# Reciprocal square roots by a GpSimd power: two LayerNorms and the output norm of a delta rule

## The chip, the cores and the metric

The kernel runs on one core of one Trainium2 chip. The metric is the device time of one execution in microseconds (us), as the median of several runs. In what follows PE is TensorE (matrix multiplications), PEld its weight loads, DVE is VectorE, ACT is ScalarE, POOL is GpSimd, and SP is SyncE, which issues nearly all DMA transfers.

## The reference, cut to what matters

One inference step of a two-layer hybrid encoder on 2048 prompt rows and 32 sample rows of width 1024. Layer 1 is a gated delta rule with 8 heads of 128, layer 2 a windowed attention with 16 query heads that share 4 key/value heads. The three places that the change concerns are the norm of the delta rule's output, per token and head, and the LayerNorm behind each layer's output projection:

```python
def layer_norm(x, g, b):
    xf = x.astype(jnp.float32)
    mu = xf.mean(-1, keepdims=True)
    var = jnp.square(xf - mu).mean(-1, keepdims=True)
    return ((xf - mu) * lax.rsqrt(var + LN_EPS) * g + b).astype(x.dtype)
...
    o, s_new = gated_delta_rule(q, k, v, g, beta, s0.astype(jnp.float32))
    o = o * lax.rsqrt(jnp.mean(o * o, -1, keepdims=True) + RMS_EPS) * norm_w * jax.nn.silu(z.astype(jnp.float32))
    out = o.reshape(b, l, A_VW).astype(x.dtype) @ w_out
    return layer_norm(DN_ALPHA * x + out, ln_g, ln_b), new_buf, s_new.astype(x.dtype)
...
    out = (o * jax.nn.silu(z)) @ w_out
    return layer_norm(DN_ALPHA * x + out, ln_g, ln_b)
```

The delta rule is solved exactly in blocks: each block needs the inverse of a unit lower triangular matrix per head, and its outputs depend on the state S that the block before left.

## The kernel before, in words

All rows are worked on in 17 tiles: 16 of 128 prompt rows and one of the 32 sample rows. Matrix products that need full accuracy are split into a high and a low part and done in three passes (lines L77 to L79 for the projections, L1089 to L1091 for the output projections); the low part of an activation or of a weight (act_lo L69, w_lo L54, g_lo L1132 and L1456) is a subtraction on POOL or VectorE.

The stages, in the order of time in the profiled execution:

- **Projection P1** (0 to about 690 us): q, k, v by blocks of 416 rows, a short convolution, and the row norms of q and k. That norm (`norms`, L423) uses the Newton iteration too and is not changed.
- **Delta rule** (class `Delta`, `run` at L803; about 690 to 1160 us): 17 chunks, one iteration of the loop over i per chunk and some 25 us each. While chunk i is finished, chunk i+1 gets its triangular inverse completed and chunk i+2 is prepared. The triangular solve of a 32x32 part is a chain of 31 steps j, each one multiplication (`tm`, L585) and one subtraction (`Tt`, L588) of small tiles: for j = 0 to 24 they run on POOL for chunk i+2 (`chain(n2, P, 0, n2.split)`), and in the next iteration VectorE does j = 25 to 30, then `spread` (L656, L657) and `invert` (L680 to L705). The state update `Sp` (L761, VectorE) stands between VectorE's chain steps, and PE's `ks` (L714) reads the new state. The output norm of chunk i is `norms` (L774): `Xo` (L778) is the mean square plus epsilon, [128 rows, 8 heads], then eleven VectorE operations give its reciprocal root `ro_y`, and `scale` (L787) multiplies the output o by it. `run` hands out the eleven one by one with `go(... r ...)` between other VectorE work such as `at` (L630) and `E` (L542). Matrix products of the remaining projection are filled in between (`fill`) until iteration 10; from iteration 11 (`OPEN`) the output projection takes their place in pieces (`side`).
- **Output projection O1** (class `OutNorm`, `tile` at L1135; most of it about 1138 to 1372 us): per tile two times 24 products of 512 columns, the residual added (L1097), `bn_stats` and `bn_aggr`, the variance plus epsilon `ve` (L1153, [128, 1]), eleven operations for `ln_y`, then two pairs of operations for the two halves of the tile: L1165 subtracts the mean and multiplies by the gain, L1167 multiplies by `ln_y` and adds the bias. PE transposes the result r (L1194) during the products of the next tile, and the copy `hT` (L1196) and a DMA put it away for the next projection.
- **Projection P2** (about 1372 to 1776 us) with the rotary embedding, and **attention** (about 1776 us to the end): per chunk scores `S` (L1559), a softmax whose exponentials P are made on ACT (L1442) and multiplied on POOL (L1567), transposes (L1574), the output products `ot` (L1580), and `finish` (L1449): output projection, `ve` (L1473), eleven Newton operations, `nb` (L1477, VectorE), r times rstd plus nb on ACT (L1478), then gain and bias on POOL (L1479, L1480) and the DMA to the output (L1488). For the very last tile, the gain and bias steps are on VectorE instead (L1484, L1486).

The Newton iteration for the reciprocal square root is eleven operations that each need the one before:

```python
    V.tensor_scalar(out=y[:n].bitcast(I32), in0=x[:n].bitcast(I32), scalar1=1, scalar2=None,
                    op0=ALU.logical_shift_right)
...
    V.tensor_scalar(out=y[:n].bitcast(I32), in0=y[:n].bitcast(I32), scalar1=-1, scalar2=0x5F3759DF,
                    op0=ALU.mult, op1=ALU.add)
...
    for _ in range(3):
        V.scalar_tensor_tensor(out=t[:n], in0=x[:n], scalar=-0.5, in1=y[:n], op0=ALU.mult, op1=ALU.mult)
        V.tensor_tensor(out=t[:n], in0=t[:n], in1=y[:n], op=ALU.mult)
        V.scalar_tensor_tensor(out=y[:n], in0=t[:n], scalar=1.5, in1=y[:n], op0=ALU.add, op1=ALU.mult)
```

What sets the order: every engine works through its own list in order and waits at each instruction for the semaphores of its inputs. In the delta rule and O1 the lists of PE and VectorE (and ACT's in the delta rule) are as `run` and `tiles` write them. POOL's and SP's lists, and all lists of the attention, are put in order by a scheduler when the program is built. A changed instruction can therefore move others on POOL, SP and ACT.

Of the kernel before, what the change touches and what calls it, by code (L numbers as in the profile page):

```python
# [10 lines left out]
F32 = mybir.dt.float32  # L11
# [3 lines left out]
ALU = mybir.AluOpType  # L15
# [416 lines left out]
def newton_steps(nc, pool, x, y, n, w, tag):  # L432

    V = nc.vector
    t = pool.tile([128, w], F32, tag=tag + "_t", name=tag + "_t")
    V.tensor_scalar(out=y[:n].bitcast(I32), in0=x[:n].bitcast(I32), scalar1=1, scalar2=None,
                    op0=ALU.logical_shift_right)
    yield
    V.tensor_scalar(out=y[:n].bitcast(I32), in0=y[:n].bitcast(I32), scalar1=-1, scalar2=0x5F3759DF,
                    op0=ALU.mult, op1=ALU.add)  # L440
    yield
    for _ in range(3):
        V.scalar_tensor_tensor(out=t[:n], in0=x[:n], scalar=-0.5, in1=y[:n], op0=ALU.mult, op1=ALU.mult)
        yield
        V.tensor_tensor(out=t[:n], in0=t[:n], in1=y[:n], op=ALU.mult)
        yield
        V.scalar_tensor_tensor(out=y[:n], in0=t[:n], scalar=1.5, in1=y[:n], op0=ALU.add, op1=ALU.mult)
        yield


def rsqrt_newton(nc, pool, x, n, w, tag):
    y = pool.tile([128, w], F32, tag=tag + "_y", name=tag + "_y")
    drain(newton_steps(nc, pool, x, y, n, w, tag))
    return y


class Chunk:
    def __init__(self, t0, n):
        self.t0, self.n, self.ti, self.ready, self.pool = t0, n, t0 // 128, False, None
# [3 lines left out]
class Delta:  # L463
# [310 lines left out]
    def norms(self, ch):  # L774


        V, n, X = self.nc.vector, ch.n, ch.X
        V.scalar_tensor_tensor(out=X[:n], in0=X[:n], scalar=1.0 / 128, in1=self.G["eq"][:n, ch.ti, :], op0=ALU.mult,  # L778
                               op1=ALU.add)
        yield  # L780
        ch.r = self.two.tile([128, 8], F32, tag="ro_y", name="ro_y")
        yield from newton_steps(self.nc, self.sml, X, ch.r, n, 8, "ro")

    def scale(self, ch):
        n = ch.n
# [318 lines left out]
class OutNorm:  # L1104


    def __init__(self, tc, es, name, side, I, pre, banks, kept):
        self.nc = nc = tc.nc
        self.one = new_pool(tc, es, name + "_one", 1, side=side)
        self.two = new_pool(tc, es, name + "_two", 2, side=side)  # L1110
        self.pp = new_pool(tc, es, name + "_pp", banks, PSUM, side=side)
        self.tabs = None
        self.tables = lambda: ln_tables(nc, self.one, I[pre + "_ln_g"], I[pre + "_ln_b"])
        self.rest = load_part_weights(nc, self.one, self.two, I[pre + "_w_out"], kept, nc.vector)
        self.w = next(self.rest)
# [19 lines left out]
    def tile(self, parts, r, n, tail=False):  # L1135

        nc, V = self.nc, self.nc.vector
        ghi, glo = parts
        st = self.two.tile([128, 2, 6], F32, tag="st", name="st")
        w = self.w  # L1140
        for c in range(2):
            cs = slice(c * 512, c * 512 + 512)
            ps = self.pp.tile([128, 512], F32, tag="po", name="po")
            for k in range(KC):
                out_products(nc, ps, ghi, glo, w, k, cs, n)
                if k % 2 == 1:
                    yield (4 if n <= 64 else 6) * 0.227
            add_products(nc, r, glo, ps, cs, n)
            V.bn_stats(out=st[:n, c, :], in_=r[:n, cs])
        mv = self.two.tile([128, 2], F32, tag="mv", name="mv")  # L1150
        V.bn_aggr(out=mv[:n], in_=st[:n])
        ve = self.two.tile([128, 1], F32, tag="ve", name="ve")
        V.tensor_scalar(out=ve[:n], in0=mv[:n, 1:2], scalar1=LN_EPS, scalar2=None, op0=ALU.add)  # L1153
        rs = rsqrt_newton(nc, self.two, ve, n, 1, "ln")
        tabs = self.tabs
        if not tail:
            nb = self.two.tile([128, 1], F32, tag="nb", name="nb")
            V.scalar_tensor_tensor(out=nb[:n], in0=mv[:n, 0:1], scalar=-1.0, in1=rs[:n], op0=ALU.mult, op1=ALU.mult)
            nc.scalar.activation(r[:n], r[:n], AF.Identity, bias=nb[:n, 0:1], scale=rs[:n, 0:1])
            nc.gpsimd.tensor_tensor(out=r[:n], in0=r[:n], in1=tabs[0][:n], op=ALU.mult)  # L1160
            nc.gpsimd.tensor_tensor(out=r[:n], in0=r[:n], in1=tabs[1][:n], op=ALU.add)
        else:
            for c in range(2):
                cs = slice(c * 512, c * 512 + 512)
                V.scalar_tensor_tensor(out=r[:n, cs], in0=r[:n, cs], scalar=mv[:n, 0:1], in1=tabs[0][:n, cs],  # L1165
                                       op0=ALU.subtract, op1=ALU.mult)
                V.scalar_tensor_tensor(out=r[:n, cs], in0=r[:n, cs], scalar=rs[:n, 0:1], in1=tabs[1][:n, cs],  # L1167
                                       op0=ALU.mult, op1=ALU.add)
        yield r


class O1:
    def __init__(self, tc, es, I, O, T, G):
        self.nc, self.I, self.T, self.G = tc.nc, I, T, G
        self.on = OutNorm(tc, es, "o1", "left", I, "a", 2, T["wo"])
        self.bank = lambda: self.on.pp.tile([128, 512], F32, tag="po", name="tr")
        self.steps = 0
        self.room = lambda: self.on.one.tile([128, KC, 128], F32, tag="g", name="hT")
# [196 lines left out]
class Attention:  # L1375
# [73 lines left out]
    def finish(self, t0, n, graw, late=False, tail=False):  # L1449
        nc, V, pool = self.nc, self.nc.vector, self.otwo  # L1450
        r = pool.tile([128, D], F32, tag="r", name="r")
        nc.sync.dma_start(r[:n], self.T["h"][t0:t0 + n, :])
        ghi = pool.tile([128, KC, 128], F32R, tag="g_hi", name="g_hi")
        glo = pool.tile([128, KC, 128], F32R, tag="g_lo", name="g_lo")
        nc.scalar.copy(ghi[:, :, :n], graw[:, :, :n])
        nc.gpsimd.tensor_tensor(out=low_part(ghi, glo, n), in0=graw[:, :, :n], in1=ghi[:, :, :n], op=ALU.subtract)  # L1456
        st = pool.tile([128, 2, 6], F32, tag="st", name="st")
        w, tabs = self.w, self.tabs
        both = self.scores_tile() if late else None
        for c in range(2):  # L1460
            cs = slice(c * 512, c * 512 + 512)
            if late:
                ps = both[:, c].rearrange("p u k -> p (u k)")
            else:
                ps = self.pp.tile([128, 512], F32, tag="po", name="po")[:]
            for k in range(KC):
                out_products(nc, ps, ghi, glo, w, k, cs, n)
            add_products(nc, r, glo, ps, cs, n)
            V.bn_stats(out=st[:n, c, :], in_=r[:n, cs])
        mv = pool.tile([128, 2], F32, tag="mv", name="mv")  # L1470
        V.bn_aggr(out=mv[:n], in_=st[:n])
        ve = pool.tile([128, 1], F32, tag="ve", name="ve")
        V.tensor_scalar(out=ve[:n], in0=mv[:n, 1:2], scalar1=LN_EPS, scalar2=None, op0=ALU.add)  # L1473
        rs = rsqrt_newton(nc, pool, ve, n, 1, "ln")
        if not tail:
            nb = pool.tile([128, 1], F32, tag="nb", name="nb")
            V.scalar_tensor_tensor(out=nb[:n], in0=mv[:n, 0:1], scalar=-1.0, in1=rs[:n], op0=ALU.mult, op1=ALU.mult)  # L1477
            nc.scalar.activation(r[:n], r[:n], AF.Identity, bias=nb[:n, 0:1], scale=rs[:n, 0:1])  # L1478
            nc.gpsimd.tensor_tensor(out=r[:n], in0=r[:n], in1=tabs[0][:n], op=ALU.mult)  # L1479
            nc.gpsimd.tensor_tensor(out=r[:n], in0=r[:n], in1=tabs[1][:n], op=ALU.add)  # L1480
        else:
            for c in range(2):
                cs = slice(c * 512, c * 512 + 512)
                V.scalar_tensor_tensor(out=r[:n, cs], in0=r[:n, cs], scalar=mv[:n, 0:1], in1=tabs[0][:n, cs],  # L1484
                                       op0=ALU.subtract, op1=ALU.mult)
                V.scalar_tensor_tensor(out=r[:n, cs], in0=r[:n, cs], scalar=rs[:n, 0:1], in1=tabs[1][:n, cs],  # L1486
                                       op0=ALU.mult, op1=ALU.add)
        nc.sync.dma_start(self.O["y"][t0:t0 + n, :], r[:n])  # L1488
# [244 lines left out]
def make_consts(tc, I, pool):  # L1733
    nc = tc.nc
    G = {}
    G["ident"] = pool.tile([128, 128], F32, tag="ident", name="ident")
    nc.sync.dma_start(G["ident"][:], I["ident"])
    for name in ("hn", "eq", "ekd", "egl", "ngc"):
        G[name] = pool.tile([128, NTT, H], F32, tag=name, name="t_" + name)
    return G  # L1740
# [126 lines left out]
```

## Time and profile before

| | |
|---|---|
| time, median of 3 runs | 2205.87 us (2204.95 to 2206.77) |
| the profiled execution's own time | 2205.77 us |
| span of its instructions | 2204.0 us |
| mean granted TensorE clock | 0.989 |
| busy: PE, VectorE, ScalarE, GpSimd | 98%, 62%, 42%, 38% of the span |

The span runs from the first instruction to the last; what lies around it is 1.8 us here. A row of a timeline reads: start, duration, engine, line, operation, output <- inputs, shape, and in brackets the idle time of the engine just before, with what ended it. Matrix products are pipelined and their ends are modelled, so a PE that counts as busy isn't always at its peak.

### The profile page before, as it was taken

How to read it: one execution, taken by the hardware profiler on the slowest of the kernel's cores; microseconds unless marked ns; L12 is line 12 of the kernel's file. 1: busy time of each engine (PE TensorE's matmuls, PEld its weight loads, DVE VectorE, ACT ScalarE, POOL GpSimd, SP SyncE). 2: the span in 40 equal slices, each digit the busy share in tenths (PEclk: the TensorE clock that was granted, in tenths of full speed). 3: DMA queues.
4: the chain of work that ended last, by engine and by line, in shares of the span. 5: the costliest groups of instructions: out<-in, count | busy, mean ns of one | idle time of the engine just before them, and what ended most of it. 6: DMA issues, size and time to landing. Idle time of an engine off the chain costs nothing.

```text
span 2204.0 us, 36640 instructions
## 1 busy us (share of the span) xinstructions
PE 2152.8 (98%) x13706; PEld 1984.2 (90%) x13706; DVE 1372.1 (62%) x2696; ACT 917.4 (42%) x2303; POOL 843.1 (38%) x1189
## 2 busy tenths in 40 slices
PE   8999999999999999999999999999999999999997
PEld 6999999999999899998888788999999986788884
DVE  3676666754366688888868875135442236668774
ACT  4444344433323677877831213222112245444541
POOL 1422212222211378878811201056441215556563
PEclk9999999999999999999999999999999999999999
DMA  5212222333354344447427764374221287233311
GB/s 197 68 59 79 67 78 68 99 110 95 107 156 144 101 148 137 133 131 238 165 94 220 224 194 145 98 239 161 68 74 66 85 197 236 79 103 97 106 63 53
DMA packets 250530, 274.48 MB, mean 125 GB/s; under 512 B 76096, under 2 KB 195200, under 8 KB 250080
## 3 DMA queue, kind: packets, MB, share of 16 engines
q1 hardware_dynamic: 238352, 248.84, 37.0%
q10 hardware_dynamic: 12000, 23.30, 3.0%
q8 instruction: 108, 1.77, 0.3%
q14 instruction: 70, 0.57, 0.1%
HBM read 168.53 MB, written 103.92 MB: 124 GB/s over the span
## 4 chain that ended last, share of the span: by engine, by line
PE 89%; POOL 3%; DMA 3%; DVE 2%; ACT 2%; issue 1%; ACTq 0%; SPq 0%; DVEq 0%; POOLq 0%
PE ps L77 17%; PE ps L79 17%; PE ps L78 17%; PE po L1089 5%; PE po L1091 5%; PE po L1090 5%; PE ot L1580 4%; PE S L1559 2%; PE tr L1574 2%; POOL Tt L588 1%; POOL tm L585 1%; PE g L562 1%; PE vp L725 1%; PE op L739 1%; PE ks L714 1%
## 5 line engine op out<-in xcount | busy, mean ns | idle before, releaser
L77 PE MATMUL ps<-act_hi,w_hi 128*128 128x416 f32 x2000 | 706.3, 354 | 2.7 <-ACT w_hi L53 1.5
L79 PE MATMUL ps<-act_hi,w_lo 128*128 128x416 f32 x2000 | 704.5, 353 | 2.4 <-POOL w_lo L54 1.2
L78 PE MATMUL ps<-act_lo,w_hi 128*128 128x416 f32 x2000 | 701.2, 351 | 0.2 <-DVE act_lo L69 0.2
L77 PEld LDWEIGHTS ps<-act_hi,w_hi 128*128 128x128 f32 x2000 | 376.6, 188 | 7.8 <-ACT w_hi L53 2.4
L79 PEld LDWEIGHTS ps<-act_hi,w_lo 128*128 128x128 f32 x2000 | 375.8, 188 | 7.2 <-POOL w_lo L54 1.7
L78 PEld LDWEIGHTS ps<-act_lo,w_hi 128*128 128x128 f32 x2000 | 376.1, 188 | 5.1 <-DVE act_lo L69 0.9
L54 POOL TENSOR_TENSOR w_lo<-w_raw,w_hi 128x1024 fp32r<-128x1024 f32 x44 | 117.0, 2660 | 472.3 <-ACT w_hi L53 446.2
L196 DVE SCALAR_TENSOR_TENSOR y<-R,convw,y 128x2083 f32<-128x2083 f32 x72 | 173.7, 2414 | 109.4 <-ACT y L194 85.0
L585 POOL TENSOR_TENSOR tm<-L,Tt 128x60 f32<-128x60 f32 (+19 forms) x373 | 139.3, 374 | 89.8 <-PE sp L755 42.9
L1567 POOL TENSOR_TENSOR P<-P,sm 128x384 f32<-128x384 f32 (+2 forms) x128 | 101.6, 814 | 177.6 <-DVE sm L1446 100.6
L588 POOL TENSOR_TENSOR Tt<-Tt,tm 128x60 f32<-128x60 f32 (+19 forms) x373 | 157.2, 421 | 29.2
L1442 ACT ACTIVATE P<-S,nm 128x192 f32<-128x192 f32 (+2 forms) x260 | 104.7, 419 | 94.2 <-DVE nm L1435 41.4
L227 ACT COPY R<-ps 128x416 f32<-128x416 f32 (+1 forms) x144 | 61.2, 448 | 197.5 <-PE ps L79 173.0
L1089 PE MATMUL po<-wo_hi,g_hi 128*128 128x512 f32 x256 | 104.8, 410 | 1.8 <-ACT hT L1196 1.8
L1286 POOL TENSOR_TENSOR rs<-rs,sin 128x416 f32<-128x416 f32 x50 | 71.1, 1421 | 80.0 <-DVE rs L1285 73.4
L1090 PE MATMUL po<-wo_lo,g_hi 128*128 128x512 f32 x256 | 101.1, 395 | 0.0
L1091 PE MATMUL po<-wo_hi,g_lo 128*128 128x512 f32 x256 | 101.0, 395 | 0.0
L1580 PE MATMUL ot<-pt,vd 128*128 128x256 f32 x372 | 98.7, 392 | 1.9 <-ACT pt L1576 1.4
L1089 PE MATMUL po<-wo,g_hi 128*128 128x512 f32 x240 | 99.4, 414 | 0.0
L53 ACT CAST w_hi<-w_raw 128x1024 fp32r<-128x1024 f32 x48 | 50.3, 1049 | 116.8 <-PE ps L78 88.2
L1091 PE MATMUL po<-wo,g_lo 128*128 128x512 f32 x240 | 96.2, 401 | 0.0
L1090 PE MATMUL po<-wo,g_hi 128*128 128x512 f32 x240 | 96.1, 400 | 0.0
(306 smaller groups left out, 4024.2 us busy)
## 6 DMA issues: line engine op xcount, KB each, us to landing
w_raw<-in_w_in SPq DMA_DIRECT2D x40, 512.0 KB
w_raw<-in_b_w_in SPq DMA_DIRECT2D x20, 512.0 KB
gb<-s_gcum SPq DMA_DIRECT2D x17, 512.0 KB
k<-s_k SPq DMA_DIRECT2D x17, 512.0 KB
s_bz<-za SPq DMA_DIRECT2D x40, 208.0 KB
s_bq<-ra SPq DMA_DIRECT2D x40, 208.0 KB
s_q<-y SPq DMA_DIRECT2D x8, 1024.0 KB
s_k<-y SPq DMA_DIRECT2D x8, 1024.0 KB
```

The costliest lines, as they stand in the source:

```text
L54: sub.tensor_tensor(out=lo[:], in0=raw[:], in1=hi[:], op=ALU.subtract)
L77: nc.tensor.matmul(ps, hi[:, k, :], xh[:, k, :], start=(k == 0), stop=False)
L78: nc.tensor.matmul(ps, hi[:, k, :], xl[:, k, :], start=False, stop=False)
L79: nc.tensor.matmul(ps, lo[:, k, :], xh[:, k, :], start=False, stop=(k == KC - 1))
L196: nc.vector.scalar_tensor_tensor(out=y[:], in0=R[:, j:j + W], scalar=self.convw[:, i, j:j + 1], in1=y[:], op0=ALU.mult, op1=ALU.add)
L585: P.tensor_tensor(out=tm[:n, i0 - k:, :w], in0=L[:n, i0:, j:j + 1].to_broadcast(sh), in1=Tt[:n, j:j + 1, :w].to_broadcast(sh), op=ALU.mult)
L588: P.tensor_tensor(out=Tt[:n, i0:, :w], in0=Tt[:n, i0:, :w], in1=tm[:n, i0 - k:, :w], op=ALU.subtract)
L1089: nc.tensor.matmul(ps[:n], ghi[:, k, :n], w[0][:, k, cs], start=a, stop=False)
L1090: nc.tensor.matmul(ps[:n], ghi[:, k, :n], w[1][:, k, cs], start=False, stop=False)
L1091: nc.tensor.matmul(ps[:n], glo[:, k, :n], w[0][:, k, cs], start=False, stop=z)
L1442: nc.scalar.activation(P[u], src, AF.Exp, bias=nm[:, u:u + 1], scale=1.0, accum_out=sm[:, u:u + 1])
L1580: nc.tensor.matmul(ot[:, p], self.vd[:, kc0 + j, p, :], pt[:, 2 * j:2 * j + 2, :], start=(j == 0), stop=(j == nj - 1))
```

## The change: what it does

A function `root` is added, one GpSimd operation that raises x to the power -0.5. The exponent comes from a tile `half` that is filled once at the start. Three callers use it in place of the Newton iteration: `Delta.norms` (17 times, [128, 8]), `OutNorm.tile` (17 times, [128, 1]) and `Attention.finish` (17 times, [128, 1]). So 51 x 11 VectorE operations go and 51 POOL operations come. In the delta rule the result is no longer handed out in steps: the later `go(r)` calls of `run` find an empty generator. The tile's name changes from `ln_y` to `rs` in the two LayerNorms; in the delta rule it stays `ro_y`. The Newton iteration of P1's `norms` stays.

```diff
+def root(nc, G, out, x):
+
+    nc.gpsimd.tensor_tensor(out=out, in0=x, in1=G["half"][:x.shape[0], 0:x.shape[1]], op=ALU.pow)
...
         V.scalar_tensor_tensor(out=X[:n], in0=X[:n], scalar=1.0 / 128, in1=self.G["eq"][:n, ch.ti, :], op0=ALU.mult,
                                op1=ALU.add)
+        ch.r = self.two.tile([128, 8], F32, tag="ro_y", name="ro_y")
+        root(self.nc, self.G, ch.r[:n], X[:n])
         yield
-        ch.r = self.two.tile([128, 8], F32, tag="ro_y", name="ro_y")
-        yield from newton_steps(self.nc, self.sml, X, ch.r, n, 8, "ro")
...
         V.tensor_scalar(out=ve[:n], in0=mv[:n, 1:2], scalar1=LN_EPS, scalar2=None, op0=ALU.add)
-        rs = rsqrt_newton(nc, self.two, ve, n, 1, "ln")
+        rs = self.two.tile([128, 1], F32, tag="rs", name="rs")
+        root(nc, self.G, rs[:n], ve[:n])
...
         V.tensor_scalar(out=ve[:n], in0=mv[:n, 1:2], scalar1=LN_EPS, scalar2=None, op0=ALU.add)
-        rs = rsqrt_newton(nc, pool, ve, n, 1, "ln")
+        rs = pool.tile([128, 1], F32, tag="rs", name="rs")
+        root(nc, self.G, rs[:n], ve[:n])
...
+    G["half"] = pool.tile([128, H], F32, tag="half", name="half")
+    nc.gpsimd.memset(G["half"][:], -0.5)
```

The second and third pair are those of `OutNorm.tile` and of `Attention.finish`; `OutNorm` also gets G handed in by `O1`.

More of the change, by code (lines that the diff above doesn't have):

```diff
@@ L1104, with __init__ @@
 class OutNorm:
-    def __init__(self, tc, es, name, side, I, pre, banks, kept):
-        self.nc = nc = tc.nc
+    def __init__(self, tc, es, name, side, I, pre, banks, kept, G):
+        self.nc, self.G = tc.nc, G
+        nc = tc.nc
         self.one = new_pool(tc, es, name + "_one", 1, side=side)
@@ L1174, in __init__ @@
         self.nc, self.I, self.T, self.G = tc.nc, I, T, G
-        self.on = OutNorm(tc, es, "o1", "left", I, "a", 2, T["wo"])
+        self.on = OutNorm(tc, es, "o1", "left", I, "a", 2, T["wo"], G)
         self.bank = lambda: self.on.pp.tile([128, 512], F32, tag="po", name="tr")
```

## The prediction, made before the changed kernel was run

> **What bounds the kernel now.** I read the page first, then the windows by stage, the chain of waits inside the delta rule, and the timelines of VectorE (DVE) and GpSimd (POOL) where the change cuts in. The page:
>
> ```profile
> span 2204.0 us, 36640 instructions
> ...
> PE 2152.8 (98%) x13706; PEld 1984.2 (90%) x13706; DVE 1372.1 (62%) x2696; ACT 917.4 (42%) x2303; POOL 843.1 (38%) x1189
> ...
> PE 89%; POOL 3%; DMA 3%; DVE 2%; ACT 2%; issue 1%; ACTq 0%; SPq 0%; DVEq 0%; POOLq 0%
> ```
>
> TensorE sets the end nearly everywhere, so 51 x 11 small VectorE operations removed are worth nothing as busy time. The 3% of POOL on the chain of waits matters more, since POOL receives the new work. The windows (columns: busy time of PE, PEld, DVE, ACT, POOL, then the TensorE clock) say where each stands:
>
> ```profile
> 865.00:890.00 25.00, 25.00 (x274) 23.99 (x274) 22.00 (x52) 20.02 (x63) 19.75 (x49) 1.00 0.44 136
> 1015.00:1040.00 25.00, 23.87 (x276) 22.52 (x274) 20.98 (x50) 21.62 (x71) 20.48 (x54) 1.00 0.61 197
> 1040.00:1065.00 25.00, 22.33 (x248) 21.30 (x248) 21.23 (x52) 20.26 (x62) 20.87 (x53) 0.93 0.61 199
> 1065.00:1090.00 25.00, 20.86 (x248) 19.69 (x248) 21.65 (x55) 20.95 (x70) 20.91 (x53) 1.00 0.61 214
> 1860.00:2000.00 140.00, 139.22 (x759) 109.25 (x759) 95.52 (x275) 64.94 (x251) 79.17 (x66) 1.00 0.32 87
> 2000.00:2150.00 150.00, 150.00 (x857) 122.06 (x854) 118.57 (x322) 74.91 (x286) 92.02 (x75) 1.00 0.30 87
> ```
>
> In delta iterations 0 to 10 (first row, one iteration of 25 us) PE is full. In 11 to 14 it is not, up to 4.1 us short per 25. What holds it there, by the chain of waits for 1005 to 1110 and by the waits of 1010 to 1115 (total, times, longest):
>
> ```profile
> by line: POOL Tt L588 29.6%; POOL tm L585 28.8%; issue 10.0%; PE vp L725 5.2%; PE ks L714 2.7%; PE gq L629 2.3%; ACT kd L601 2.0%; PE g L562 1.9%; ACT nb L567 1.4%; PE vtr L612 1.4%; ACT vn L771 1.2%; ACT vn L615 1.1%; PE bps L686 1.0%; PE
> ```
> ```profile
> PE ks L714 <- DVE Sp L761: 6.0, 4, 2.0
> DVE tm L585 <- POOL Tt L588: 5.7, 4, 1.7
> ```
>
> POOL's 25-step solve (L585/L588) runs chain after chain; VectorE's last steps wait for its end, the state update Sp is queued behind those on VectorE, and PE waits for Sp. A POOL instruction added here moves the end.
>
> **Part 1: the delta rule's output norm (17 times, [128,8]).** Iteration 6 and the start of 7 on POOL, and the VectorE row that needs the chain:
>
> ```profile
> 868.45 0.26 POOL L585 TENSOR_TENSOR tm<-L,Tt 128x31 f32<-128x31 f32 x1 [1.57 <-ACT vn L771]
> ...
> 871.15 0.30 POOL L588 TENSOR_TENSOR Tt<-Tt,tm 128x28 f32<-128x28 f32 x1
> ...
> 892.36 0.29 POOL L588 TENSOR_TENSOR Tt<-Tt,tm 128x49 f32<-128x49 f32 x1
> 893.50 0.26 POOL L585 TENSOR_TENSOR tm<-L,Tt 128x31 f32<-128x31 f32 x1 [0.85 <-DVE tm L585]
> ```
> ```profile
> 893.24 0.17 DVE L585 TENSOR_TENSOR tm<-L,Tt 128x42 f32<-128x42 f32 x1
> ```
>
> In the changed program's POOL order the power stands inside the chain: after its 14th pair in iterations 1 to 10, within the 11th pair in 11 to 14, after all chains in 15 and 16. Its price is in no row. Below I put 0.25 us, since the smallest POOL TENSOR_TENSOR here lasts 0.26 to 0.30; above 3.3 us, as if POOL did the eleven steps one by one at 0.30. I take 1.0 us for 128x8, near the middle of these two ends in ratio (the square root of 0.25 x 3.3 is 0.9), and 0.55 for 128x1; with the gap of about 0.07 between POOL instructions, 1.07.
>
> Iterations 0 to 10: the chain of iteration 6 ends at 892.65, and VectorE takes it at 893.24. The two idle gaps, 1.57 and 0.85, average 1.21 us per iteration. 1.07 fits, narrowly: **0**. Above a price of about 1.15 us it no longer does, and POOL becomes the bound of all eleven iterations.
>
> Iterations 11 to 14:
>
> ```profile
> 1024.03 0.14 DVE L778 SCALAR_TENSOR_TENSOR Xo<-Xo,t_eq 128x8 f32<-128x8 f32 x1
> ...
> 1024.94 0.28 DVE L436 TENSOR_SCALAR ro_y<-Xo 128x8 int32<-128x8 int32 x1
> ...
> 1026.17 1.37 DVE L542 TENSOR_TENSOR E<-gb,nm 128x1024 f32<-128x1024 f32 x1
> ...
> 1028.61 1.23 DVE L787 TENSOR_TENSOR o<-o,ro_y 128x1024 f32<-128x1024 f32 x1
> ```
> ```profile
> 1017.14 0.26 POOL L585 TENSOR_TENSOR tm<-L,Tt 128x31 f32<-128x31 f32 x1 [0.45 <-ACT vn L771]
> ...
> 1026.53 1.18 POOL L585 TENSOR_TENSOR tm<-L,Tt 128x76 f32<-128x76 f32 x1
> ```
>
> VectorE loses 1028.61-1024.94-1.37 = 2.3 us of Newton steps, but it waits for POOL later in the iteration anyway: worth 0. The power's input is written at 1024.03, before its place in the chain, so POOL does not wait for it. Only 0.45 us of idle time stands before the chain of iteration 11, so iteration 10's power carries 1.07-0.45 = **+0.6** into it; the chains of 11, 12 and 13 add 1.07 each, **+3.2**; that of 14 is partly covered, because PE's own late sp is waited for next: **+0.5**. Sum +4.3.
>
> The second POOL row shows a cost that stays: beside E on VectorE it lasts 1.18 us where its neighbours last 0.3. The Trainium skill, "SBUF — State Buffer", section "SBUF: two separate sides", says that GpSimd and a VectorE operation with two SBUF inputs hold a shared pair of ports exclusively, the other blocking fully. The trace agrees (1.18 against 0.3); by that rule a power caught behind E, o or k could last some 0.9 us longer, an estimate that would make the delta sum about +7.
>
> **Part 2: LayerNorm of the output projection (17 times, [128,1]).** Tile 2, where the P2 weight split also sits on POOL:
>
> ```profile
> 1173.23 0.14 DVE L1153 TENSOR_SCALAR ve<-mv 128x1 f32<-128x1 f32 x1
> ...
> 1175.34 0.16 DVE L447 SCALAR_TENSOR_TENSOR ln_y<-ln_t,ln_y 128x1 f32<-128x1 f32 x1
> ...
> 1177.64 0.75 DVE L1167 SCALAR_TENSOR_TENSOR r<-r,ln_y,ln_b 128x512 f32<-128x512 f32 x1
> 1178.31 1.22 DVE L1132 TENSOR_TENSOR g_lo<-g,g_hi 128x1024 fp32r<-128x1024 f32 x1
> ...
> 1179.85 2.40 POOL L54 TENSOR_TENSOR w_lo<-w_raw,w_hi 128x1024 fp32r<-128x1024 f32 x1 [67.85 <-ACT w_hi L53]
> ```
> ```profile
> 1180.95 0.60 PE L1194 MATMUL ps<-ident,r 128*128 128x128 f32 x4
> ```
>
> In the new POOL order w_lo stands ahead of tile 2's power. It waits for its data until 1179.85 and lasts 2.40, so the power can't start before 1182.3 although ve is ready at 1173.4. Root at 1182.9, the first half of r at 1183.7, all of it at about 1185.1 instead of 1178.4; g_lo and the add that frees a PSUM bank are queued behind it on VectorE. PE's transposes of r, at 1180.95 now, start 2.7 (first half enough) to 4.2 us late: **+3.5**. Tile 3's power stands behind the second w_lo, beside which one Newton step lasts 2.3 us already: even. Tile 5's stands behind an activation split on POOL; PE's second transposes of that tile wait today:
>
> ```profile
> 1216.20 2.27 POOL L69 TENSOR_TENSOR act_lo<-act_raw,act_hi 128x832 fp32r<-128x832 f32 x1 [3.05 <-ACT act_hi L68]
> ```
> ```profile
> 1219.16 0.63 PE L1194 MATMUL ps<-ident,r 128*128 128x128 f32 x4 [0.75 <-DVE r L1167]
> ```
> ```profile
> 1240.00:1372.00 132.00, 131.44 (x655) 112.03 (x655) 97.36 (x224) 30.01 (x47) 14.13 (x9) 1.00 0.58 180
> ```
>
> The split ends at 1218.5, root at 1219.1, r at 1221.3: 2 us behind today's transposes if the split moves along with tile 2's delay, and nothing if it does not, as PE is then 3.5 us later itself: **+1**. From 1240 on PE is full, POOL nearly idle: 0. Sum +4.5.
>
> **Part 3: LayerNorm of the attention (17 times) and the tail.** From 2000 to 2150 PE is full. From 1860 to 1930 the chain of waits is:
>
> ```profile
> by line: PE ot L1580 21.8%; PE S L1559 17.4%; PE po L1089 14.8%; PE po L1090 13.6%; PE po L1091 13.3%; PE tr L1574 12.2%; DVE nm L1435 2.4%; ACT P L1442 2.4%; DVE nm L1434 1.4%; ACT pt L1576 0.7%; issue 0.5%; ACTq L1442 0.1%
> ```
>
> VectorE and ScalarE hold 6.3% of 70 us, 4.4 us, of which a shorter VectorE queue may give back some: I take **-1**. The bound is what 1860 to 2000 would save at the weight-load density of 2000 to 2150: 140 - 109.25/(122.06/150) = 5.7 us. On the other side, nb waits on VectorE for a power that may stand behind POOL's products; at one 2.4 us POOL instruction a time in the two or three chunks not yet full of PE, up to +5.
>
> The tail, on POOL, SP and VectorE:
>
> ```profile
> 2175.36 2.38 POOL L1456 TENSOR_TENSOR g_lo<-graw,g_hi 128x1024 fp32r<-128x1024 f32 x1
> 2177.70 2.84 POOL L1480 TENSOR_TENSOR r<-r,ln_b 128x1024 f32<-128x1024 f32 x1
> ...
> 2183.26 0.32 SPq L1452 DMA_DIRECT2D r<-s_h  x1
> ...
> 2195.33 0.15 DVE L1473 TENSOR_SCALAR ve<-mv 128x1 f32<-128x1 f32 x1
> 2195.40 1.40 DVE L1484 SCALAR_TENSOR_TENSOR r<-r,mv,ln_g 128x512 f32<-128x512 f32 x2
> 2196.72 0.14 DVE L436 TENSOR_SCALAR ln_y<-ve 128x1 int32<-128x1 int32 x1
> ...
> 2198.83 1.42 DVE L1486 SCALAR_TENSOR_TENSOR r<-r,ln_y,ln_b 128x512 f32<-128x512 f32 x2
> ```
>
> At the end, the power runs beside L1484 (1.40) instead of 2.1 us of Newton after it: -1.4 after a handover, up to -2. Earlier, the last chunk's g_lo moves behind the two POOL steps of the chunk before, so r<-s_h can be issued sooner: about -1.5. **-2.9** (0 to -4).
>
> **Sum.** +4.3 +4.5 -1 -2.9 = +4.9, on the profiled execution's 2205.77 us, which agrees with the median of 2205.87: **2210.7 us**.
>
> **Rivals.**
> A. The power costs 2 us or more, and POOL bounds the whole delta rule. Against the 1.21 us of idle time: 11 x (2.07-1.21) = 9.5, iterations 11 to 14 with the carry 3.5 x 2.07+0.7 = 8, O1 5, tail -1.5: +21, 2227; at 3.3 us, 23.8+12.5+6.5-0.5 = +42, 2248. For it: a power is no multiply, and no row prices it. Against: 2 us for 8 columns is nearly seven times what POOL takes for a product of 28 (0.30). A sentence apart: the Trainium skill, "GPSIMD Engine Reference", section "Instruction dispatch", gives about 6 us for the first call of a freshly loaded kernel; no run here shows it, and it would add an estimated 5 us once.
> B. The other side: attention is relieved in full (-5.7), the tail gives -3.5, a power of 0.35 us costs the delta 3.5 x 0.42 = +1.5, and w_lo's data come early enough that tile 2 pays nothing: 2198. It decides by whether PE's weight loads in 1860 to 2000 become as dense as later, 0.81 busy against 0.78. Against it: PE already counts as busy for 139.22 of 140.
> C. It cancels: a power near 0.5 us (delta +2), tile 2 at +2.7, tail -3.5, attention 0: about 2207.
>
> **How the numbers follow.** What the measurement can tell from no change is about 0.2%, 4.4 us: 2201.5 to 2210.3, and my sum lies just above its upper edge. Chances: forecast with its own range 2206 to 2217, 0.38; A 0.27; B 0.13; C 0.22. Above the bound lie all of A, some 0.22 of the forecast's case and 0.01 of C: slower 0.50. Below lie B and 0.05 of C: faster 0.18. The rest: same 0.32. The range reaches into B and A: 2199 to 2236.
>
> **What would show it.** The POOL rows of the power give its price. In iterations 11 to 14, chain starts on POOL should stand 1.0 us or so further apart than 24; in 0 to 10 the period should stay 25.0 (wider: A). PE's transposes of tile 2 should wait 3 to 4 us, with w_lo ahead of the power. The weight-load share of 1860 to 2000 decides B. In the tail, the last L1484 and L1486 should follow each other closely. The forecast is wrong if the price misses 0.6 to 1.2 us, or if PE's waits appear where I saw it full.

## The result, and the profile after

| | median | runs |
|---|---|---|
| before | 2205.41 us | 2204.21 to 2206.77 (4) |
| changed | 2223.50 us | 2221.95 to 2228.78 (4) |

The ratio is 1.0083 (1.0066 to 1.0100): the change costs 18.1 us. The profiled execution of the changed kernel is the slowest of its four (2228.78 us, mean TensorE clock 0.987), so the stage lengths are shown from a second profile of it too, that of e1 (2221.46 us, 0.992).

The page of the changed kernel, the lines that answer to those of before:

```profile
span 2227.0 us, 36148 instructions
...
PE 2166.9 (97%) x13706; PEld 1987.5 (89%) x13706; DVE 1282.7 (58%) x2135; ACT 918.0 (41%) x2303; POOL 881.7 (40%) x1241
...
PE 84%; POOL 5%; DMA 4%; DVE 3%; ACT 2%; issue 2%; SPq 1%; ACTq 0%; DVEq 0%; POOLq 0%
```

VectorE lost 89 us of busy time, and PE's share of the chain fell from 89% to 84%: the removed work was hardly on the path, and waits came onto it. The power itself, grouped by shape:

```profile
L459 POOL TENSOR_TENSOR rs<-ve,half x34: 540/547/992, 1142.8 to 2220.7; 128x1 f32<-128x1 f32 x32, 32x1 f32<-32x1 f32 x2
...
L459 POOL TENSOR_TENSOR ro_y<-Xo,half x17: 1637/1647/2729, 752.9 to 1159.1; 128x8 f32<-128x8 f32 x16, 32x8 f32<-32x8 f32 x1
```

(Numbers after the colon: shortest, median, longest in ns, then first and last start.) 1.65 us for eight columns, 0.55 for one: if a straight line holds between these two sizes, some 0.16 us a column on a base of 0.39 (an estimate). I had assumed 1.0 and 0.55.

Where the time went is read from the same VectorE rows in each trace: `Xo` of the delta rule, and `ve` of the two LayerNorms, whose first and last starts group as follows, before and then changed:

```profile
L1153 DVE TENSOR_SCALAR ve<-mv x17: 141/153/155, 1138.5 to 1345.5; 128x1 f32<-128x1 f32 x16, 32x1 f32<-32x1 f32 x1
```
```profile
L1159 DVE TENSOR_SCALAR ve<-mv x17: 142/154/156, 1142.6 to 1358.4; 128x1 f32<-128x1 f32 x16, 32x1 f32<-32x1 f32 x1
...
L1480 DVE TENSOR_SCALAR ve<-mv x17: 132/147/154, 1879.2 to 2220.4; 128x1 f32<-128x1 f32 x16, 32x1 f32<-32x1 f32 x1
```

| stretch (us) | before | changed | changed, e1 | alone |
|---|---|---|---|---|
| delta, Xo of iteration 10 to 16 | 152.3 | 155.3 | 152.6 | 153.1 (e2) |
| O1, first ve to last | 207.0 | 215.9 | 215.1 | 214.6 (e3) |
| attention, 7th ve to 13th | 130.0 | 137.6 | 137.6 | 137.6 (e4) |
| 13th ve to the end | 71.7 | 69.3 | 69.2 | 69.3 (e4) |

Kernels whose delta rule is that of before show 148.7 to 152.5 in the first row, so a single profile can't price that stage to better than some 3 us; the timed runs do. Most of this spread lies in the last of the six intervals: 22.7 us in the five of these profiles whose granted clock was 1.00 from 1128 to 1155 us, 25.9 to 27.2 in the four where it was 0.87 or 0.88 there (before is one of these). In the second row, kernels with Newton in O1 show 204.5 to 207.6, so before's own 207.0 lies high; the third row is clear. In O1 the power waits behind other POOL work. POOL of the changed kernel, and the VectorE rows of tiles 2, 5 and 8 that use the root:

```profile
1181.64 2.66 POOL L54 TENSOR_TENSOR w_lo<-w_raw,w_hi 128x1024 fp32r<-128x1024 f32 x1 [16.83 <-ACT w_hi L53]
1184.25 0.55 POOL L459 TENSOR_TENSOR rs<-ve,half 128x1 f32<-128x1 f32 x1
...
1220.16 1.98 POOL L69 TENSOR_TENSOR act_lo<-act_raw,act_hi 128x832 fp32r<-128x832 f32 x1 [3.25 <-ACT act_hi L68]
1222.10 0.54 POOL L459 TENSOR_TENSOR rs<-ve,half 128x1 f32<-128x1 f32 x1
...
1260.92 1.98 POOL L69 TENSOR_TENSOR act_lo<-act_raw,act_hi 128x832 fp32r<-128x832 f32 x1 [2.77 <-ACT act_hi L68]
1262.86 0.54 POOL L459 TENSOR_TENSOR rs<-ve,half 128x1 f32<-128x1 f32 x1
```
```profile
1184.84 0.75 DVE L1174 SCALAR_TENSOR_TENSOR r<-r,rs,ln_b 128x512 f32<-128x512 f32 x1 [2.79 <-POOL rs L459]
...
1222.68 0.75 DVE L1174 SCALAR_TENSOR_TENSOR r<-r,rs,ln_b 128x512 f32<-128x512 f32 x1 [5.22 <-POOL rs L459]
...
1263.43 0.75 DVE L1174 SCALAR_TENSOR_TENSOR r<-r,rs,ln_b 128x512 f32<-128x512 f32 x1 [4.73 <-POOL rs L459]
```

The bracket is VectorE idle: 2.8, 5.2 and 4.7 us, with the add (L1102) that frees PE's PSUM bank queued behind each. The other tiles wait 0.44 or 0.45 us.

In the attention no such wait explains 7.6 us; PE's own order is another. The score products S of before and of the changed kernel, on PE:

```profile
2040.15 1.57 PE L1559 MATMUL S<-kT,qs 64*128 64x192 f32 x16
2041.65 1.56 PE L1580 MATMUL ot<-pt,vd 128*128 128x256 f32 x6
```
```profile
2058.77 0.59 PE L1567 MATMUL S<-kT,qs 64*128 64x192 f32 x4
2059.30 0.55 PE L1582 MATMUL tr<-ident,P 128*128 128x128 f32 x3
```

From S to the next instruction: 16 records in 1.50 us, 94 ns each, before; 4 in 0.53 us, 133 ns each, after. In the list that the scheduler wrote for PE, and in PE's rows of the traces, the score products of the prompt's chunks stand in 53 unbroken groups before and in 68 after.

### The profile page after: what moved, and what is told of

Its sections match the earlier page's. It is cut to its first block, busy times and chain, and to the rows that moved or that the text cites. A ratio compares the mean times of both kernels' runs of the same rounds, so it can differ in the third digit from the quotient of the medians.

```text
span 2227.0 us, 36148 instructions
## 1 busy us (share of the span) xinstructions
PE 2166.9 (97%) x13706; PEld 1987.5 (89%) x13706; DVE 1282.7 (58%) x2135; ACT 918.0 (41%) x2303; POOL 881.7 (40%) x1241
## 4 chain that ended last, share of the span: by engine, by line
PE 84%; POOL 5%; DMA 4%; DVE 3%; ACT 2%; issue 2%; SPq 1%; ACTq 0%; DVEq 0%; POOLq 0%
PE ps L77 17%; PE ps L79 16%; PE ps L78 16%; PE po L1094 4%; PE po L1096 4%; PE po L1095 4%; PE ot L1588 4%; PE S L1567 2%; POOL tm L590 2%; POOL Tt L593 2%; DMA act_raw<-s_hT 2%; PE tr L1582 2%; PE g L567 1%; PE vp L730 1%; PE op L744 1%
## 5 line engine op out<-in xcount | busy, mean ns | idle before, releaser
L590 POOL TENSOR_TENSOR tm<-L,Tt 128x60 f32<-128x60 f32 (+19 forms) x373 | 133.9, 359 | 76.6 <-ACT vn L776 44.8
L593 POOL TENSOR_TENSOR Tt<-Tt,tm 128x60 f32<-128x60 f32 (+19 forms) x373 | 149.1, 400 | 28.8
```

What stands on the lines that cost most here:

```text
L590: P.tensor_tensor(out=tm[:n, i0 - k:, :w], in0=L[:n, i0:, j:j + 1].to_broadcast(sh), in1=Tt[:n, j:j + 1, :w].to_broadcast(sh), op=ALU.mult)
L593: P.tensor_tensor(out=Tt[:n, i0:, :w], in0=Tt[:n, i0:, :w], in1=tm[:n, i0 - k:, :w], op=ALU.subtract)
```

## The experiments

All were timed in turn with the kernel before on the same chip. The table gives each median, that of before beside it, and the ratio with its 95% interval.

| | kernel | median | before | ratio |
|---|---|---|---|---|
| e1 | the whole change again | 2223.15 | 2204.53 | 1.0080 (1.0067 to 1.0094) |
| e2 | delta rule alone | 2207.65 | 2204.53 | 1.0011 (1.0002 to 1.0020) |
| e3 | O1 alone | 2214.63 | 2204.53 | 1.0039 (1.0025 to 1.0053) |
| e4 | attention alone | 2210.08 | 2204.53 | 1.0026 (1.0016 to 1.0037) |
| e5 | last three LayerNorms of the attention | 2197.01 | 2205.48 | 0.9967 (0.9954 to 0.9980) |
| e6 | attention with no root at all | 2215.67 | 2205.48 | 1.0057 (1.0037 to 1.0077) |
| e7 | attention: Newton, and a power unused | 2203.44 | 2205.48 | 0.9996 (0.9984 to 1.0008) |
| e8 | O1 but for tiles 2, 5, 8 | 2205.45 | 2205.48 | 1.0002 (0.9993 to 1.0012) |
| e9 | delta rule, power doubled | 2215.62 | 2207.33 | 1.0048 (1.0030 to 1.0066) |
| e10 | delta rule with no root | 2205.06 | 2207.33 | 0.9993 (0.9981 to 1.0005) |
| e11 | O1 with no root | 2202.09 | 2207.33 | 0.9978 (0.9968 to 0.9988) |
| e12 | first six and last three of the attention | 2198.27 | 2207.33 | 0.9959 (0.9943 to 0.9975) |

**The three parts (e1 to e4).** In each, the two other places go back to Newton, for instance

```diff
-        rs = self.two.tile([128, 1], F32, tag="rs", name="rs")
-        root(nc, self.G, rs[:n], ve[:n])
+        rs = rsqrt_newton(nc, self.two, ve, n, 1, "ln")
```

> The whole change once more, on the same chip as its three parts. About 2222 us if the first profiled execution (2228.8) was a few us above the others; the three parts should then sum to about +17 if they are independent.

> The power in the delta rule alone, Newton in both LayerNorms. Theory 1, from the offsets of the changed trace: nothing in iterations 0 to 10 although the power takes 1.65 us, because it covers one of the blocked 1.18 us steps, and +3 in 11 to 16: about 2209. Theory 2, the rival A of the prediction: POOL is the bound of all iterations, 11 x (1.72-1.21) more: about 2215.

> The power in the output projection's LayerNorm alone. Theory 1: three powers (tiles 2, 5, 8) wait behind w_lo and act_lo on POOL, PE loses 1.5+1.8+4 there and 1 to 2 where the next projection starts: about 2214. Theory 2, the loss came from upstream delays that meet the weights' DMA: less than half of it, about 2208.

> The power in the attention's LayerNorm alone. Its order of PE breaks the score products into 68 groups where before has 53. Theory 1: this order costs what the changed trace lost between 2027 and 2131, about 9 us, and the tail gives 3.6 back: about 2211. Theory 2: that loss was a wait handed down from upstream or a clock that differed in that one execution, and only the tail's gain is left: about 2202.

By the ratios on 2205 us the parts cost 2.4 (0.4 to 4.4), 8.6 (5.5 to 11.7) and 5.7 us (3.5 to 8.2), 16.7 together, against 17.6 for the whole: they add up, and the times are those of theory 1 in each. POOL is not the bound of the early delta iterations, O1 is the largest part, and the attention costs by itself, on an undisturbed start. In one thing e3 is not as expected: its tile 2 pays next to nothing. VectorE's rows for tiles 2, 5 and 8, and PE's two long waits, in e3:

```profile
1175.39 0.75 DVE L1174 SCALAR_TENSOR_TENSOR r<-r,rs,ln_b 128x512 f32<-128x512 f32 x1 [0.44 <-POOL rs L459]
...
1213.12 0.75 DVE L1174 SCALAR_TENSOR_TENSOR r<-r,rs,ln_b 128x512 f32<-128x512 f32 x1 [4.97 <-POOL rs L459]
...
1254.05 0.75 DVE L1174 SCALAR_TENSOR_TENSOR r<-r,rs,ln_b 128x512 f32<-128x512 f32 x1 [4.99 <-POOL rs L459]
```
```profile
1218.96 0.47 PE L1094 MATMUL po<-wo_hi,g_hi 128*128 128x512 f32 x1 [2.54 <-DVE r L1102]
...
1259.90 0.47 PE L1094 MATMUL po<-wo_hi,g_hi 128*128 128x512 f32 x1 [2.54 <-DVE r L1102]
```

Here w_lo started at 1172.00, so tile 2's power came at 1174.36 and VectorE waited 0.44 us for it. With 1.04 and 0.87 us before the transposes of tiles 5 and 8, PE's idle time at these two tiles is 7.0 us.

**O1: is it the queue? (e8, e11)**

```diff
-        rs = self.two.tile([128, 1], F32, tag="rs", name="rs")
-        root(nc, self.G, rs[:n], ve[:n])
+        if newton:
+            rs = rsqrt_newton(nc, self.two, ve, n, 1, "ln")
+        else:
+            rs = self.two.tile([128, 1], F32, tag="rs", name="rs")
+            root(nc, self.G, rs[:n], ve[:n])
...
-            for j, out in enumerate(self.on.tile(got, r, t[2], True)):
+            for j, out in enumerate(self.on.tile(got, r, t[2], True, i in (2, 5, 8))):
```

> As the power in the output projection alone, but Newton for tiles 2, 5 and 8, whose powers stood behind w_lo or act_lo. Theory 1, these three waits are the loss: 6 to 8 of the 8.6 us come back, about 2206. Theory 2, the power's own handover (0.9 to 1.2 us a tile against 2.1 of Newton) or the shifted DMAs cost: 2212 or more.

All of it came back, within 2 to 3 us. The wait of VectorE for the root falls from 16 us in O1 alone to 6 with three Newton tiles (total, times, longest; e3, then e8):

```profile
DVE r L1174 <- POOL rs L459: 16.2, 16, 5.0
```
```profile
DVE r L1177 <- POOL rs L459: 5.8, 13, 0.5
```

So these three of seventeen powers made the loss, and the other fourteen gained nothing that the interval shows (0.9993 to 1.0012). e8 changes the three together; by the waits in e3 it was two of them, tiles 5 and 8. e11 takes both forms away (`rs = ve`), the most that any replacement could give:

> Output projection's LayerNorm with neither Newton nor power: ve in place of its reciprocal root, its output left unscaled. It bounds what any replacement could give. Theory 1, PE is full there: 2203 to 2206. Theory 2, the waits of tile 5 and of the tail of O1 come back: 2200 to 2202.

The ratio is worth -4.9 us (-2.6 to -7.1): nearer to theory 2. The Newton steps of O1 are not free although PE counts as full there; a root without a queue could win some of this, which no run tried.

**Attention: power, or PE's order? (e6, e7, e5, e12)** e6 has `rs = ve`; e7 keeps Newton and adds `root(nc, self.G, dead[:n], ve[:n])`; e5 and e12 choose by tile:

```diff
-        rs = pool.tile([128, 1], F32, tag="rs", name="rs")
-        root(nc, self.G, rs[:n], ve[:n])
+        if late or t0 in (640,):
+            rs = pool.tile([128, 1], F32, tag="rs", name="rs")
+            root(nc, self.G, rs[:n], ve[:n])
+        else:
+            rs = rsqrt_newton(nc, pool, ve, n, 1, "ln")
```

with six more values of t0 in e12.

> Attention's LayerNorm with neither Newton nor power: ve is used in place of its reciprocal root, so its output is left unscaled. PE's order breaks the score products into 73 groups. Theory 1, the order of PE is what costs: as much or more lost than with the power in the attention alone (2210), some 2209 to 2214, although no power runs. Theory 2, the power's wait or price costs: nothing lost and the tail's gain, about 2201.

> Newton kept everywhere, and a power on POOL beside it in the attention whose result nothing uses. PE's order is that of before (53 groups). Theory 1: about 2205 to 2207, only POOL's 17 x 0.55 to 0.9 us more, mostly beside other work. Theory 2: the 9 us are lost as in the changed kernel, and no tail gain: about 2214.

> The power in the last three LayerNorms of the attention alone, Newton everywhere else; PE's order is that of before (53 groups of score products), POOL's order at the end that of the changed kernel. If the tail's gain stands on its own: 3.6 us, about 2201, which would be below both kernels. If it was only the shadow of delays before it: 2204 to 2205.

> The power in nine LayerNorms of the attention (the first six and the last three), Newton in the other eight; PE's order keeps 53 groups of score products. Theory 1, the power in itself costs nothing in the attention, only the changed order of PE does: as with the last three alone, about 2197 to 2200. Theory 2, each power in the attention costs: 6/14 of the 9 us come back as loss, about 2202 to 2204.

Without any power, but with 73 groups, the attention loses more (e6); with all seventeen powers on POOL, their results unused, and 53 groups it loses nothing (e7). With nine powers in use and 53 groups it is faster than before (e12), but none of these nine lies in the stretch from the 7th to the 13th LayerNorm, so for that stretch e6 and e7 decide. What reorders PE is the shorter VectorE list, not the new POOL work: e6 has no power and is the most broken, and e7 has every power and PE's order of before. A shorter list doesn't always reorder it: with three or nine LayerNorms changed (e5, e12) there are still 53 groups.

The length of a group sets its time, in the kernel before as well. There too four products between other work take 0.53 us:

```profile
1898.99 0.59 PE L1559 MATMUL S<-kT,qs 64*128 64x192 f32 x4
1899.52 0.55 PE L1574 MATMUL tr<-ident,P 128*128 128x128 f32 x3
```

Eight take 0.85 us, twelve 1.18, sixteen 1.50, in before and in e4 alike, for products of 192 columns wherever PE doesn't wait and the clock is full. (Some records of matrix products can be missing, so a group of two that takes 0.52 us may be one of four.) From the 7th to the 13th `ve`, before has 12 groups, all of 16, and e4 has 26. One of the 26 holds the only wait of PE in this stretch, for VectorE's `pt`:

```profile
2054.55 0.92 PE L1566 MATMUL S<-kT,qs 64*128 64x192 f32 x8
2056.97 0.52 PE L1581 MATMUL tr<-ident,P 128*128 128x128 f32 x3 [1.50 <-DVE pt L1585]
```

Each PE row taken from its start to the next one's, the stretch adds up so, before and in e4: score products 18.0 and 23.6 us, transposes 12.4 and 14.1, output projection 70.2 and 71.4, `ot` 29.0 and 28.1. So 5.6 of the 7.6 us stand at the score products, 1.5 of them as that wait and 4.1 as the price of shorter groups. Why a short group costs more per product stays open, and no run put PE's list of before under the power in all seventeen LayerNorms.

e5 and e12 are the versions that beat both kernels. At the end of e5:

```profile
2193.32 0.15 DVE L1479 TENSOR_SCALAR ve<-mv 128x1 f32<-128x1 f32 x1
2193.39 1.40 DVE L1494 SCALAR_TENSOR_TENSOR r<-r,mv,ln_g 128x512 f32<-128x512 f32 x2
2193.55 1.00 POOL L459 TENSOR_TENSOR rs<-ve,half 128x1 f32<-128x1 f32 x1 [3.32 <-DVE ve L1479]
2194.71 1.41 DVE L1496 SCALAR_TENSOR_TENSOR r<-r,rs,ln_b 128x512 f32<-128x512 f32 x2
```

The power lies under the 1.40 us that VectorE needs anyway. From the 13th ve to the end e5 takes 67.4 us against 71.7: 4.3 of the 7.3 us (4.4 to 10.1) that the ratio gives, 2.1 of them from the last ve on; the rest was not traced to a row.

**Delta rule (e9, e10).** e9 adds a second `root` of the same input into a tile that nothing reads; e10 has `ch.r = X`.

> As the power in the delta rule alone, with a second power of the same input beside it whose result nothing uses. POOL's idle time left in iterations 0 to 10 with one power is about 0.8 us per iteration. Theory 1, the second costs its 1.65 in full on POOL: 0.8 x 11 + 1.65 x 3.5 = 15 more than with one, about 2222. Theory 2, it too covers a blocked 0.9 us step: hardly anything in 0 to 10, some 2.5 in 11 to 14, about 2210.

> Delta rule with neither Newton nor power: Xo itself is the factor, so the outputs are scaled wrongly. Theory 1, the Newton steps are worth nothing there since VectorE waits for POOL later in the iteration: 2203 to 2206. Theory 2, the freed 2.3 us of VectorE shorten iterations 11 to 16: 2198 or less.

e10 is theory 1: the Newton steps were worth nothing there that the interval (0.9981 to 1.0005) shows. e9 lies between its two theories: by the difference of the ratios of e9 and e2, the second power costs 8.2 us (0.37%), not 15 and not 3. In its trace the period stays 25 us while the power starts ahead of E, and grows by 0.5 to 1.3 us once POOL is late enough for E to start first; the power is then blocked as well. POOL in the early iterations and later, and E beside the later one:

```profile
830.90 1.64 POOL L459 TENSOR_TENSOR ro_y<-Xo,half 128x8 f32<-128x8 f32 x1
...
907.23 2.62 POOL L459 TENSOR_TENSOR ro_y<-Xo,half 128x8 f32<-128x8 f32 x1
```
```profile
907.03 1.32 DVE L547 TENSOR_TENSOR E<-gb,nm 128x1024 f32<-128x1024 f32 x1
```

## Why the prediction was right in direction and range, and wrong in size

Forecast was +4.9 us, measured +18.1. The direction and the range, 2199 to 2236, held; the mechanism of the forecast made only part of the time. That the range held is partly luck: its upper part stood there for rival A, a POOL that bounds the delta rule, and was filled by the attention and by two tiles of O1 that I had at +1 and 0.

- **Delta rule, +4.3 forecast, +2.4 (0.4 to 4.4) measured.** The price failed (1.65 us instead of 1.0), and by my own threshold of 1.15 POOL should then have bound iterations 0 to 10, which is rival A. It didn't. The iteration around 880 us of the changed kernel shows why, on POOL and on VectorE (it is 5 counted by `Xo` from 0, as in the table; the prediction calls it 6):

```profile
880.57 1.64 POOL L459 TENSOR_TENSOR ro_y<-Xo,half 128x8 f32<-128x8 f32 x1
882.17 0.31 POOL L590 TENSOR_TENSOR tm<-L,Tt 128x68 f32<-128x68 f32 x1
882.56 1.19 POOL L593 TENSOR_TENSOR Tt<-Tt,tm 128x68 f32<-128x68 f32 x1
...
894.63 0.26 POOL L590 TENSOR_TENSOR tm<-L,Tt 128x31 f32<-128x31 f32 x1 [0.44 <-DVE tm L590]
```
```profile
880.61 1.24 DVE L547 TENSOR_TENSOR E<-gb,nm 128x1024 f32<-128x1024 f32 x1
```

  E runs beside the power and stops nothing; before, such an operation blocked a chain step for 0.9 us. That holds for iterations 3, 5, 7 and 9. In 1, 2, 4, 6 and 8 of the changed kernel E starts first, by 0.03 to 0.23 us, and the power itself lasts 2.64 to 2.73 us, for instance in iteration 6:

```profile
905.57 1.23 DVE L547 TENSOR_TENSOR E<-gb,nm 128x1024 f32<-128x1024 f32 x1
```
```profile
905.61 2.68 POOL L459 TENSOR_TENSOR ro_y<-Xo,half 128x8 f32<-128x8 f32 x1
```

  The period stays 25 us even so. Over two iterations (893.50 to 943.36 us before, 894.63 to 944.54 changed) POOL is busy 39.80 and 41.86 us, and the two powers take 4.33 of the latter: 2.3 us of POOL's other work and 2.0 us of its idle time made room for them. With the power in the delta rule alone (e2), most idle times at the chains' starts in these iterations are 0.45 or 1.19 us, against 0.84 or 1.57 before. I had counted the blocked steps as a cost that stays; some of them are a cover that the power moves into. The Trainium skill, "SBUF — State Buffer", section "SBUF: two separate sides", says that whichever of the two starts first holds the ports for its whole instruction. Measured: with E first the power is stretched (2.68 us here, 2.62 in e9), as the rule says; with the power first by 0.04 us both take their usual time (1.64 and 1.24), so there the power did not keep E out for its whole length.
- **Iterations 11 to 14** have the mechanism that was named, at half the size. PE's wait for Sp grows from 6.0 to 7.2 us (8.0 in e1 and e2) and VectorE waits up to 2.5 instead of 1.7 (rows below). But from the start of the chain at 1017 us to the start of the third one after it, e1 and e2 take 73.0 to 73.1 us where kernels with Newton in the delta rule take 71.3 to 71.9: some 1.5 us, where the sum had 3.2 at the lower price of 1.07. So the +4.3 came near the +2.4 by two errors that offset each other, a price too low and a share of it too high.

```profile
PE ks L719 <- DVE Sp L766: 7.2, 4, 2.9
...
DVE tm L590 <- POOL Tt L593: 5.9, 3, 2.5
```

- **O1, +4.5 forecast, +8.6 (5.5 to 11.7) measured.** The mechanism, a power queued behind other POOL work, is shown by e8; the places were wrong. Tile 2 carried +3.5 of the sum. In the whole change its power comes at 1184.25 behind w_lo as described, but PE idles only 0.3 and 0.8 us there, and in e3 VectorE waits 0.44. Tile 5 was taken as +1 and its VectorE wait is 5.2 us (5.0 in e3); tile 8, which I set to 0 under "from 1240 on PE is full", waits 4.7 (5.0). I looked at PE's share and not at each power's neighbour in POOL's list, where the act_lo ahead of tile 8's stood to be read.
- **Attention, -1 forecast, +7.6 measured between the 7th and the 13th LayerNorm.** This is the step that failed. I took the edit's price from VectorE's queue and POOL's, with PE's list as given. In this stage the scheduler writes PE's list too, and it wrote another one: 26 groups of score products in place of 12 in that stretch. The text on the order of lists says that a changed instruction can move others on POOL, SP and ACT; in the attention it moved PE's too. None of the rivals held this. (The 6.3% that the prediction gives VectorE and ScalarE there leaves out ACT's `pt`; with it the line says 7.0%. Nothing turned on it.)
- **Tail, -2.9 forecast.** -2.4 in the whole change, -4.3 in e5, where PE's order is intact. From the last `ve` to the end the time falls from 8.65 to 6.54 us: the power under L1484, right with its mechanism. The other term, -1.5 for an earlier r<-s_h, has only 0.3 us left for it in the whole change and 2.2 in e5, where it was not told apart.
- **Rival B** was wrong in its condition: PE's weight loads in 1860 to 2000 stayed at 108.99 of 140 us, against 109.25 before (109.12 from 1875 to 2015, since the attention starts 15 us later there). Its other side, a kernel at about 2198, is what e5 and e12 reach (2197.0 and 2198.3), more than half of it in the tail:

```profile
1860.00:2000.00 140.00, 139.00 (x753) 108.99 (x753) 84.34 (x208) 63.70 (x244) 75.54 (x67) 1.00 0.31 86
```

- **A first call's cost**, which the prediction quotes from the Trainium skill, "GPSIMD Engine Reference", section "Instruction dispatch", as about 6 us for a freshly loaded kernel, does not appear. POOL had run other TENSOR_TENSOR operations by then, so whether this power is such a first call isn't shown. It starts at 752.94, 0.14 us after its input, and lasts 1.65:

```profile
752.94 1.65 POOL L459 TENSOR_TENSOR ro_y<-Xo,half 32x8 f32<-32x8 f32 x1 [3.53 <-DVE Xo L783]
```

## What to carry to other kernels

Where a scheduler writes an engine's list, compare the new list with the old one on every engine, the bound one first: an edit that takes work off an idle engine can reorder the full one, and that can cost more than the work did. A short operation moved to a queue is priced by what stands ahead of it there at each place; three bad places of seventeen, and by the waits two of these, made the loss in O1. Put the offloaded step only where it lies under other work and delays no one, here the end of the kernel.

## What the runs showed of the hardware that was not expected

A GpSimd power of 128x8 lasts 1.64 us, of 128x1 0.54, and 32x8 takes as long as 128x8 (1.65). Its 128x1 form lasts 0.92 to 1.0 where the VectorE operation on r, with two inputs, starts just before it, as in tile 0 of O1:

```profile
1142.65 0.74 DVE L1172 SCALAR_TENSOR_TENSOR r<-r,mv,ln_g 128x512 f32<-128x512 f32 x1
1142.81 0.99 POOL L459 TENSOR_TENSOR rs<-ve,half 128x1 f32<-128x1 f32 x1 [7.91 <-DVE ve L1159]
```

The score products with 64 rows of weights and 192 columns run at 94 ns each in a group of 16, 106 in a group of 8 and 132 in a group of 4, in the kernel before as in the changed one.
